# Inputs of VectorE moved to PSUM and a gate product moved to ScalarE, in the second part of a decoder block

## The chip, the core and the metric

One core of a Trainium2 chip. The time is the device time of one execution in microseconds (us); of several runs the median counts. Engines: TensorE (PE in the profile, PEld its weight loads), VectorE (DVE), ScalarE (ACT), GpSimd (POOL) and SyncE (SP, which issues most DMAs).

## The reference

A decoder block of 1024 tokens with 1024 features, all in float32: adaLN modulation, an input projection, a causal convolution beside an RWKV-7 time mixing, an output projection, and then a PEER mixer of 16384 experts. The last is what the change is about:

```python
q = (xc @ w_q).reshape(tc, PEER_HEADS, 2, PEER_DQ // 2)
s = jnp.einsum('thpd,hpkd->thpk', q, sub_keys)
...
best, pos = lax.top_k(cand.reshape(tc, PEER_HEADS, ...), PEER_TOPK)
gate = jax.nn.softmax(best, axis=-1)
ue = jnp.take(expert_u, expert, axis=0)
ve = jnp.take(expert_v, expert, axis=0)
h = jax.nn.gelu(jnp.einsum('thkd,td->thk', ue, xc), approximate=False)
return jnp.einsum('thk,thkd->td', gate * h, ve)
```

Each token has 8 heads of 16 experts: 128 rows of U (1024 values) whose dot products with the token go through Gelu, are multiplied with the gate, and weigh 128 rows of V.

## The kernel before, in words

The 1024 tokens are 8 tiles of 128. The first part of the kernel (to about 1900 us) does all of the block up to the choice of the experts. For the experts there are two ways, by tile:

- Tiles 0, 3, 6 and 7 are *gathered*. `stream_fetch` asks, with an indirect DMA of GpSimd's queue, for one row of U and V (2048 values) per token, 128 times per tile, into three buffers (`row`). `stream_use` makes the dot product of the U half with the tokens (`V.tensor_tensor_reduce`, shown as CUSTOM_DVE_ANT_0 and an accumulator read). `stream_add` has ScalarE make Gelu of the one column `hj`, VectorE multiply it with the gate, and VectorE add the V half times `hj` to `acc` (`scalar_tensor_tensor`, 128x1024). When that has ended, the buffer is free for a new gather. In the first part GpSimd makes a quarter of the dot products (`stream_useg`). After 128 rows, the tile's end transposes `acc` on TensorE into the bank `pD`, adds the residual and normalises.
- Tiles 1, 2, 4 and 5 (512 tokens) are *dense*: in the second part they go through all experts on TensorE. There are 128 blocks of 128 experts. Each operand is split into a high and a low part (type F32R), and each product is three matmuls: high by high, low by high and high by low. `stream_du` splits a block of U (`wh` on ScalarE, `wl` on GpSimd), `stream_dv` pieces of V (`vh`, `vl` likewise). `stream_mm` makes 24 matmuls of 512 columns into a bank `ph` (two of them); `stream_post` makes Gelu on ScalarE into `h` in SBUF, two products with the gates `gt` on VectorE, `ch` (ScalarE) and `cl` (VectorE); after 4 blocks `stream_mm` makes the 8 products with V, 12 matmuls each, into banks `po` (four of them), and `stream_sum` adds each to `accT` in SBUF on VectorE. The rows of the gathered tiles that are left (some 280 of 512) run beside it.

The streams are Python generators. `Issue.go` takes the stream whose next instruction can start first by a rough estimate; a `Wait` holds a stream back until a condition on the streams' counters holds. So the order of the instructions on each engine is fixed when the program is built. A tile with `bufs=n` takes its place from the n-th tile before, and waits on the chip until that one has been read.

[...] In the second part `pD` and `pC` have one each, `ph` two and `po` four.

Nearly all profile rows have the line L220, the helper that issues every operation; the names of the tiles tell them apart.

Of the kernel before, what the change touches and what calls it, by code (L numbers as in the profile page):

```python
# [19 lines left out]
T = 1024  # L20
D = 1024
# [7 lines left out]
def _groups():  # L29
    """The pairs (a, b) of ranks that can be among the 16 best sums, as rectangles (a0, na, b0, nb), in the order in  # L30
    which they are laid out: a pair has at least (a + 1)(b + 1) - 1 pairs before it that are not less, so that only
    those with (a + 1)(b + 1) <= 16 count, and among the 8 best are only those with (a + 1)(b + 1) <= 8."""
    out, ends, n = [], [], 0
    for lo, hi in ((0, TOPK // 2), (TOPK // 2, TOPK)):
        for a in range(hi):
            b0, b1 = lo // (a + 1), hi // (a + 1)
            if b0 == b1:
                continue
            if out and len(ends) == (lo > 0) and out[-1][2:] == [b0, b1 - b0] and out[-1][0] + out[-1][1] == a:
                out[-1][1] += 1  # L40
            else:
                out.append([a, 1, b0, b1 - b0])
            n += b1 - b0
        ends.append(n)
    return out, ends
# [9 lines left out]
# columns of the packed per-feature vectors  # L55
# [10 lines left out]
# tiles of 128 tokens whose experts are gathered; the others go through all experts on the tensor engine  # L66
GATHER = (0, 3, 6, 7)
GE = 4  # blocks of 128 experts whose results are added up in PSUM
RUN_EXPERTS = True
# what the issue of an instruction of a stream on an engine is put back by, in ns  # L70
# [4 lines left out]
HG = (2, 8)  # heads that are selected at a time, by tile  # L75
# by how many instructions those of a stream come before their place in the order of issue
# [3 lines left out]
HU = 2  # heads that are asked for before the tokens are put away for the experts  # L80
SHARE = 4  # of 16 experts, those whose products are GpSimd's in the first phase
# [3 lines left out]
# ---------------------------------------------------------------------------------------------------  # L85
# The order in which instructions are issued: several streams of instructions are written down as
# generators, and the stream whose next instruction can start first goes first, by a rough estimate of
# what each instruction takes. Only the order depends on the estimate.
# ---------------------------------------------------------------------------------------------------
# [87 lines left out]
class Issue:  # L177
# [56 lines left out]
    def transfer(self, ready, dur):  # L234
        """the end of a transfer in the first gap that holds it"""
# [14 lines left out]
    def go(self, streams, until=None):  # L250
        """streams: generators, the most urgent first; until: when to stop, if not at the end of all"""
# [31 lines left out]
def block_kernel(ctx, tc, xT, cols, ada_w, w_in, w0, w2a2, g2, w_out, w_q, keysT, peer_uv, peer_uT, outT, dbg=None):  # L283
# [17 lines left out]
    psumD = ctx.enter_context(tc.tile_pool(name="psumD", bufs=1, space=PSUM))  # L301
# [7 lines left out]
    psum = first.enter_context(tc.tile_pool(name="psum", bufs=1, space=PSUM))  # L309

# [15 lines left out]
    def pD():  # L326
        return tl(psumD, [128, 512], "pD", bufs=1)

# [48 lines left out]
    # cumulative sums within a chunk (s on partitions, t on the free axis), relative to the chunk's middle:  # L377
    # [s <= t - kind] - [s <= MID], kind 0 inclusive, 1 exclusive
# [15 lines left out]
    # masks of the grams: rows s (either half), columns t; 0: s < t, 1: s <= t  # L394
# [8 lines left out]
    # identity in chunk form [(c t), s]  # L403
# [3 lines left out]
    # level k of the inverse: t in the odd, s in the even half of the same block of 2^(k+1)  # L407
# [28 lines left out]
    # sigmoid(x) as (1 + tanh(x / 2)) / 2, whose table the scalar engine seldom has to change: the halves go  # L436
    # into what is multiplied with it
# [3 lines left out]
    # silu(c), each value along a row: the products with it come out on every partition  # L441
# [13 lines left out]
    # carried over the tokens  # L455
# [8 lines left out]
    def weights(src, wtag):  # L464
        """a block of weights in two pieces"""
# [37 lines left out]
    def rsqrt(out, t, x, eps):  # L503
        """out = (x + eps) ** -0.5: the table's value and one Newton step"""
# [5 lines left out]
    def mods(x, acol, shcol, n, pool, tag, ps):  # L510
        """x = rmsnorm(x) * acol + shcol in place, feature-major [128, 8, n]"""
        yield from norm(x, n, pool, tag, ps)
        yield from affine(x, acol, shcol)
# [29 lines left out]
    # ================= stream A: input projection and conv =================  # L543
    def stream_a():
        # the norm of the first tokens while the modulations are on their way
# [14 lines left out]
    def macro_a(t0, n, u):  # L560
# [19 lines left out]
        # blocks (wl|al), k0-3, r0-3, v0-3, gl with the token shift  # L580
        for m, b in enumerate((12, 4, 5, 6, 7, 0, 1, 2, 3, 8, 9, 10, 11, 13)):
            ps = yield from proj(b)
            # mu times the tokens, after the one before
# [12 lines left out]
        # gated input of the conv: blocks a_i, b_i  # L596
# [12 lines left out]
    # ================= stream L: conv, layer norm, silu =================  # L609
# [38 lines left out]
    # the taps of the conv, channel block by channel block: on the tensor engine as diagonal matrices, on the  # L648
    # scalar engine and GpSimd, or on the vector engine
# [42 lines left out]
    # ================= stream B: rwkv, 128 tokens at a time =================  # L692
# [8 lines left out]
    def have(i, n):  # L701
        """whether the first n blocks of the input projection are there for tile i"""
# [3 lines left out]
    def rwkv_tile(i):  # L706
# [18 lines left out]
        # cumulative decays  # L725
# [17 lines left out]
        # kk normalised per head  # L743
# [13 lines left out]
        # k * (1 + (a - 1) k_a)  # L757
# [8 lines left out]
        # alpha | rho and beta | kappa (chunk 1: kappa | beta)  # L766
# [9 lines left out]
        # grams: rows (beta|kappa), columns (alpha|rho)  # L776
# [20 lines left out]
        # token-major copies: v, beta|kappa, alpha  # L797
        UV = [rt("UV%d" % c, ("Pn", "Px")[c], (128, NH, 64)) for c in range(2)]

        def copies():  # L800
            for c in range(2):
                k0 = 64 - 64 * c
                pt = pB((128, 512))
                for p in range(4):
                    o, vi = pt[k0:k0 + 64, p * 128:(p + 1) * 128], v[:, p, c * C:(c + 1) * C]
                    if k0:  # a transpose can't write from partition 64 on
# [18 lines left out]
            # bonus  # L825
# [19 lines left out]
        # (I - L)^-1, both chunks at once, in blocks that double  # L845
# [29 lines left out]
        # M V, Z = T M V, W^T = alpha^T T^T  # L875
# [23 lines left out]
        # the chain over chunks  # L899
# [24 lines left out]
        # group norm per head, bonus, gate  # L924
# [21 lines left out]
    # ================= stream C: output projection, selection of the experts =================  # L946
# [10 lines left out]
    def macro_c(t0, n):  # L957
# [4 lines left out]
        if not t0:  # L962
            # the part of the conv, while the rwkv part is on its way
# [71 lines left out]
    # ================= stream D: selection =================  # L1035
# [26 lines left out]
    def top16(src, vals, idxs, n8, n):  # L1062
        """the 8 best of the first n8 values, then the 8 next of all n; overwrites src"""
# [6 lines left out]
    def select_experts(st, i, h0, hg):  # L1070
        """the experts and gates of the heads h0 .. h0 + hg - 1"""
# [5 lines left out]
        # a pair (a, b) of ranks can be among the 16 best only if (a + 1)(b + 1) <= 16  # L1077
# [56 lines left out]
    def selected(st, i):  # L1134
# [8 lines left out]
        # the selected pairs and gates with the 128 places on partitions, tokens along  # L1143
# [17 lines left out]
    # ================= stream G: gates of all experts for the tokens that aren't gathered =================  # L1161
    ONE = []  # a, b, token of the pair, whether of the late kind
    none = dict(made=[0, 0], used=[0, 0])

    def stream_g():
        for m, i in enumerate(DT_):
            yield Wait(lambda: done["sel"] > i)
            selT = SEL[i]["selT"]
            for ch in range(8):
                # in the places of stream A, once it has come to its end  # L1170
                late = int(done["yin"] == NT)
                qs = 4 if late else 2
                for t in range(16 * ch, 16 * ch + 16, qs):
# [8 lines left out]
                    # a: the gate where the first key is the place; b: 1 where the second key is,  # L1182
                    # on the scalar engine as |place - second key|, then 1 where that is 0
# [43 lines left out]
    # ================= streams of the gathered experts: fetch, products with the tokens, sums =================  # L1227
    ROW, DOT, USED, U2, X1, FIN = {}, {}, set(), {}, {}, set()
# [3 lines left out]
    def stream_fetch():  # L1232
        ring = []  # what tells whether the place of a row may be taken
# [3 lines left out]
        for m, i in enumerate(GT_):  # L1237
# [9 lines left out]
            # a place for the end of the tile  # L1247
# [6 lines left out]
    def stream_use():  # L1254
        """products of the experts with the tokens on the vector engine"""
        for m, i in enumerate(GT_):
# [3 lines left out]
            for n in range(m * 128, (m + 1) * 128):  # L1260
                yield Wait(lambda: done["fetch"] > n)
                if OWN[n]:
                    continue
                hj = tl(gat, [128, 1], "hj", bufs=2 * ROWS)
                row = ROW[n][:, 0:1024]
                yield V.tensor_tensor_reduce(row, row, U2[m], 1.0, 0.0, ALU.mult, ALU.add, hj)
# [3 lines left out]
    def stream_useg():  # L1270
        """the same on GpSimd and the scalar engine, for a part of the experts of the first phase"""
# [11 lines left out]
    def stream_add():  # L1283
        for m, i in enumerate(GT_):
            acc = None
            for j in range(128):
                n = m * 128 + j
                yield Wait(lambda: n in DOT and SEL[i].get("gates", 0) > j)
                if acc is None:
                    acc = tl(gat, [128, 8, 128], "acc")  # L1290
                    accf = acc.rearrange("p k t -> p (k t)")
# [4 lines left out]
                yield V.tensor_tensor(hj, hj, gate[:, j:j + 1], op=ALU.mult)  # L1296
                if j:
                    yield V.scalar_tensor_tensor(accf, row, hj, accf, op0=ALU.mult, op1=ALU.add)
                else:
                    yield V.tensor_scalar(accf, row, hj, None, op0=ALU.mult)  # L1300
                USED.add(n)
                done["used"] = n + 1
            # x + gt_ffn * out, feature-major, and the last norm
            yield Wait(lambda: done["x1"] > m)
            x1, sq = X1[m][:, 0], X1[m][:, 1]
            yield lock()
            done["lock"] = 1
            for h in range(2):
                ps = pD()
# [7 lines left out]
            ps = pD()  # L1317
# [254 lines left out]
```

## Time and profile before

| | |
|---|---|
| median of 3 runs | 3683.55 us (3681.07 to 3698.7) |
| span of the profiled execution | 3691.2 us; no other time of it is given |
| PE busy in the span | 3158.9 us, 86% |
| DVE | 3293.1 us, 89% |
| ACT | 1439.0 us, 39% |
| POOL | 2272.8 us, 62% |
| DMA | 923.02 MB, mean 250 GB/s |

Busy is the time in which the engine had an instruction under way, also one that stood still inside. The shares are of the whole span, which has two parts of a different kind: they have to be read per part, with the windows.

### The profile page before, as it was taken

Reading aid. Unit: us, or ns where it says so; the run is one execution under the profiler, and the core shown is the slowest. Engines: PE = TensorE matmul, PEld = TensorE weight load, DVE = VectorE, ACT = ScalarE, POOL = GpSimd, SP = SyncE. Lnnn points to the kernel's source line nnn. Section 1 sums busy time; section 2 is a strip of 40 time slices with the busy share of each in tenths; the row PEclk is TensorE's granted clock in tenths of the full one; section 3 lists DMA queues with packets and bytes.
Section 4 is the critical chain, followed back from the end, with each engine's and each line's share of the span. In section 5 each row is a group of like instructions: output and inputs, shape, how many; then the busy total and the mean of one; then the engine's idle time right before and its main releaser. Section 6 shows DMA issues by size and latency. Waiting matters only on the chain. (4 is left out here: it accounts for less than half of the span.)

```text
span 3691.2 us, 53824 instructions
## 1 busy us (share of the span) xinstructions
PE 3158.9 (86%) x18460; PEld 2544.7 (69%) x18460; DVE 3293.1 (89%) x6356; ACT 1439.0 (39%) x3315; POOL 2272.8 (62%) x2007
## 2 busy tenths in 40 slices
PE   5999998986999799767847789889889999889897
PEld 4788787765777577656746677667667777667675
DVE  5744989799698979988999999999999999999998
ACT  3545526436553436525642222222222232222222
POOL 1304647677675655567858766666666766666664
PEclk9788997988899889868878899999999999999998
DMA  6654776864676357657886788888888888888886
GB/s 208 207 171 156 282 248 235 300 211 175 235 283 228 129 177 248 230 178 271 288 303 217 245 277 282 285 269 294 277 289 284 290 283 298 285 291 281 286 280 226
DMA packets 423938, 923.02 MB, mean 250 GB/s; under 512 B 30449, under 2 KB 263025, under 8 KB 354033
## 3 DMA queue, kind: packets, MB, share of 16 engines
q0 software_dynamic: 73728, 536.90, 41.2%
q1 hardware_dynamic: 349936, 382.67, 32.0%
q8 instruction: 147, 2.41, 0.3%
q14 instruction: 127, 1.03, 0.1%
HBM read 873.33 MB, written 46.14 MB: 249 GB/s over the span
## 5 line engine op out<-in xcount | busy, mean ns | idle before, releaser
L220 POOL DMA_INDIRECT row<-in_peer_uv_dram,idx x512 | 670.4, 1309 | 723.5 <-DVE acc L220 504.9
L220 DVE CUSTOM_DVE_ANT_0 row<-row,u 128x1024 f32<-128x1024 f32 x457 | 705.8, 1545 | 36.1 <-DMA row<-in_peer_uv_dram,idx 34.7
L220 DVE SCALAR_TENSOR_TENSOR acc<-row,hj,acc 128x1024 f32<-128x1024 f32 x508 | 720.7, 1419 | 9.2
L220 ACT ACTIVATE hj<-hj 128x1 f32<-128x1 f32 x512 | 102.9, 202 | 1123.3 <-DVE hj L220 1122.0
L220 PE MATMUL po<-ch,vl 128*128 128x512 f32 x1024 | 427.8, 420 | 127.0 <-POOL vl L220 126.8
L220 PE MATMUL po<-ch,vh 128*128 128x512 f32 x1024 | 417.8, 409 | 37.1 <-ACT vh L220 21.2
L220 PE MATMUL po<-cl,vh 128*128 128x512 f32 x1024 | 414.6, 409 | 22.6 <-DVE cl L220 21.6
L220 POOL TENSOR_TENSOR vl<-v,vh 128x512 fp32r<-128x512 f32 x256 | 369.8, 1452 | 52.3 <-ACT vh L220 49.2
L220 PE MATMUL pA<-uA,wtA 128*128 128x256 f32 (+1 forms) x1760 | 352.9, 352 | 12.3 <-ACT xs L220 5.6
L220 DVE TENSOR_TENSOR hj<-hj,gate 128x1 f32<-128x1 f32 x512 | 291.3, 571 | 77.5 <-ACT hj L220 77.2
L220 POOL TENSOR_TENSOR wl<-w,wh 128x1024 fp32r<-128x1024 f32 x128 | 327.7, 2561 | 47.1 <-ACT wh L220 45.6
L220 PEld LDWEIGHTS po<-ch,vl 128*128 128x128 f32 x1024 | 200.4, 196 | 217.3 <-POOL vl L220 178.1
L220 POOL TENSOR_TENSOR cb<-cb,tap 128x256 f32<-128x256 f32 (+1 forms) x300 | 236.8, 790 | 161.8 <-ACT tap L220 139.0
L220 PE MATMUL ph<-uh,wh 128*128 128x512 f32 x1024 | 288.8, 416 | 43.6 <-ACT wh L220 40.0
L220 PEld LDWEIGHTS pA<-uA,wtA 128*128 128x128 f32 x1760 | 291.3, 200 | 46.9 <-ACT xs L220 7.2
L220 DVE TENSOR_TENSOR h<-h,gt 128x256 f32<-128x256 f32 x256 | 277.1, 1121 | 2.5 <-ACT h L220 2.3
L220 PE MATMUL pC<-uC,wtC 128*128 128x256 f32 (+1 forms) x1280 | 265.4, 362 | 15.8 <-ACT uC L220 6.0
L220 PEld LDWEIGHTS ph<-uh,wh 128*128 128x128 f32 x1024 | 209.2, 205 | 92.8 <-ACT wh L220 41.0
L220 PE MATMUL ph<-uh,wl 128*128 128x512 f32 x1024 | 267.4, 394 | 2.7 <-POOL wl L220 2.7
L220 PE MATMUL ph<-ul,wh 128*128 128x512 f32 x1024 | 268.3, 390 | 0.0
L220 PEld LDWEIGHTS po<-ch,vh 128*128 128x128 f32 x1024 | 199.2, 195 | 97.0 <-ACT vh L220 30.1
L220 PEld LDWEIGHTS po<-cl,vh 128*128 128x128 f32 x1024 | 200.3, 196 | 75.4 <-DVE cl L220 36.6
(299 smaller groups left out, 6486.3 us busy)
## 6 DMA issues: line engine op xcount, KB each, us to landing
v<-in_peer_uv_dram SPq DMA_DIRECT2D x256, 256.0 KB
w<-in_peer_uT_dram SPq DMA_DIRECT2D x128, 512.0 KB
wtA<-in_w_in_dram SPq DMA_DIRECT2D x220, 256.0 KB
wtC<-in_w_q_dram SPq DMA_DIRECT2D x160, 256.0 KB
Gd<-stg SPq DMA_DIRECT2D x32, 1024.0 KB
gt<-Gd SPq DMA_DIRECT2D x31, 1024.0 KB
wtC<-in_w_out_dram SPq DMA_DIRECT2D x80, 256.0 KB
wtC<-in_ada_w_dram SPq DMA_DIRECT2D x64, 256.0 KB
```

Source lines behind the costliest of these rows:

```text
L220: r = op.fn(*op.a, **op.k)
```

## The change

In the second part of the program:

- The tokens of a gathered tile are copied to PSUM once (`up`, two banks), and the dot products read them there. `acc` lies in PSUM too (`ap`, two banks), read and written in place; the last of the 128 sums writes to SBUF.
- Gelu of a dense block is made in place in the bank `ph`, the gates are multiplied in place, and `ch` and `cl` are made from there. The counter `d["P"]`, on which the next but one block's matmuls wait, goes up after `cl` instead of after Gelu.
- `po` has two banks, one of its own and `pC`, and the wait for `stream_sum` is two pieces shorter. The bank `pD` belongs to the first part alone; the end of a gathered tile in the second part uses `pO` without the lock.

In both parts the product of `hj` with the gate is on ScalarE, as an activation Copy whose scale is the gate. The change also takes out comments. Its core:

```diff
+    def pO(n):
+        return pC() if n % 2 else tl(second["psum"], [128, 512], "po", bufs=1)
...
 def stream_use():
+                if second and m not in UP:
+                    UP[m] = tl(second["psum"], [128, 1024], "up")
+                    yield A.copy(UP[m], U2[m])
                 hj = tl(gat, [128, 1], "hj", bufs=2 * ROWS)
                 row = ROW[n][:, 0:1024]
-                yield V.tensor_tensor_reduce(row, row, U2[m], 1.0, 0.0, ALU.mult, ALU.add, hj)
+                yield V.tensor_tensor_reduce(row, row, UP.get(m, U2[m]), 1.0, 0.0, ALU.mult, ALU.add, hj)
...
 def stream_add():
                 yield A.activation(hj, hj, AF.Gelu)
-                yield V.tensor_tensor(hj, hj, gate[:, j:j + 1], op=ALU.mult)
+                yield A.activation(hj, hj, AF.Copy, scale=gate[:, j:j + 1])
+                old, inp = acc, second and j < 127
+                if acc is None or inp != acc[1]:
+                    acc = (tl(second["psum"], [128, 1024], "ap") if inp else tl(gat, [128, 1024], "acc"), inp)
                 if j:
-                    yield V.scalar_tensor_tensor(accf, row, hj, accf, op0=ALU.mult, op1=ALU.add)
+                    yield V.scalar_tensor_tensor(acc[0], row, hj, old[0], op0=ALU.mult, op1=ALU.add)
...
-                ps = pD()
+                ps = pO(h) if late else pD()
...
 def stream_mm():
-                    yield Wait(lambda: d["V"] > o and d["S"] >= o - 3)
+                    yield Wait(lambda: d["V"] > o and d["S"] >= o - 1)
                     vh, vl = V_.pop(o)
-                    PO[o] = ps = tl(psum2, [128, 512], "po", bufs=4)[:, :NTD]
+                    PO[o] = ps = pO(o)[:, :NTD]
...
 def stream_post():
-            h = tl(dn, [128, NTD], "h", bufs=2)
-            yield A.activation(h, PH.pop(e), AF.Gelu)
-            d["P"] = e + 1
+            h = PH.pop(e)
+            yield A.activation(h, h, AF.Gelu)
...
             yield A.copy(ch, h)
             yield V.tensor_tensor(cl, h, ch, op=ALU.subtract)
             C_[e] = (ch, cl)
-            d["C"] = e + 1
+            d["P"] = d["C"] = e + 1
```

## Rows read from the trace of the kernel before

**Rows 1.** Windows: stretch, length, busy of each engine (instructions), PE clock, DMA share, GB/s

```profile
1600.00:1900.00 300.00, 221.63 (x1310) 194.57 (x1309) 275.04 (x767) 154.24 (x330) 221.46 (x228) 0.79 0.75 268
1940.00:3672.00 1732.00, 1532.29 (x6212) 1192.73 (x6213) 1689.01 (x1946) 477.25 (x963) 1154.59 (x733) 0.96 0.83 277
2200.00:3600.00 1400.00, 1253.74 (x5163) 980.77 (x5162) 1370.64 (x1549) 389.09 (x786) 924.74 (x564) 0.97 0.85 285
```

**Rows 2.** Costliest groups by shape, DVE, 2000 to 3600 us (count | busy, mean | idle before)

```profile
L220 DVE CUSTOM_DVE_ANT_0 row<-row,u 128x1024 f32<-128x1024 f32 x276 | 466.5, 1690 | 1.9 <-DMA row<-in_peer_uv_dram,idx 1.8
L220 DVE SCALAR_TENSOR_TENSOR acc<-row,hj,acc 128x1024 f32<-128x1024 f32 x273 | 391.0, 1432 | 7.7
L220 DVE TENSOR_TENSOR h<-h,gt 128x256 f32<-128x256 f32 x240 | 259.7, 1121 | 2.5 <-ACT h L220 2.3
L220 DVE TENSOR_TENSOR hj<-hj,gate 128x1 f32<-128x1 f32 x275 | 220.9, 804 | 19.5 <-ACT hj L220 19.4
L220 DVE TENSOR_TENSOR accT<-accT,po 128x512 f32<-128x512 f32 x234 | 157.0, 679 | 0.0
L220 DVE TENSOR_TENSOR cl<-h,ch 128x512 fp32r<-128x512 f32 x120 | 106.5, 903 | 0.8 <-ACT ch L220 0.7
L220 DVE DVE_READ_ACCUMULATOR2_ANT hj<- 128x1 f32 x276 | 22.0, 80 | 0.0
...
L220 DVE SCALAR_TENSOR_TENSOR x<-pD,modc,x 128x128 f32<-128x128 f32 x16 | 4.5, 338 | 0.0
```

**Rows 3.** Timeline, 2600 to 2632 us: start, duration, instruction

```profile
2602.82 1.21 DVE L220 CUSTOM_DVE_ANT_0 row<-row,u 128x1024 f32<-128x1024 f32 x1
...
2607.46 1.28 DVE L220 SCALAR_TENSOR_TENSOR acc<-row,hj,acc 128x1024 f32<-128x1024 f32 x1
...
2609.80 0.76 DVE L220 TENSOR_TENSOR h<-h,gt 128x256 f32<-128x256 f32 x2
...
2611.47 2.78 POOL L220 TENSOR_TENSOR wl<-w,wh 128x1024 fp32r<-128x1024 f32 x1
...
2611.92 3.42 DVE L220 CUSTOM_DVE_ANT_0 row<-row,u 128x1024 f32<-128x1024 f32 x1
...
2615.86 2.86 DVE L220 TENSOR_TENSOR hj<-hj,gate 128x1 f32<-128x1 f32 x1
2616.18 2.52 POOL L220 TENSOR_TENSOR vl<-v,vh 128x512 fp32r<-128x512 f32 x2
...
2622.05 0.16 DVE L220 TENSOR_TENSOR hj<-hj,gate 128x1 f32<-128x1 f32 x1 [0.27 <-ACT hj L220]
```

**Rows 4.** The same groups, POOL, 2000 to 3600 us

```profile
L220 POOL DMA_INDIRECT row<-in_peer_uv_dram,idx x277 | 393.5, 1421 | 434.1 <-DVE acc L220 403.7 <-DVE hj L220 16.1 <-issue 5.4
L220 POOL TENSOR_TENSOR vl<-v,vh 128x512 fp32r<-128x512 f32 x242 | 349.0, 1450 | 43.2 <-ACT vh L220 40.3
```

**Rows 5.** Waits, 2000 to 3600 us: who for whom, total us, times, longest

```profile
POOL row L220 <- DVE acc L220: 403.7, 198, 6.3
...
PE po L220 <- POOL vl L220: 121.5, 103, 3.8
```

**Rows 6.** Windows of 10 us, columns as in group 1

```profile
2490.00:2500.00 10.00, 9.59 (x42) 7.52 (x41) 9.93 (x14) 2.87 (x6) 5.45 (x4) 1.00 1.03 375
...
2640.00:2650.00 10.00, 10.00 (x45) 8.25 (x45) 10.00 (x13) 4.27 (x9) 4.24 (x3) 1.00 0.65 218
```

**Rows 7.** Groups by shape, DVE, 0 to 1900 us

```profile
L220 DVE TENSOR_TENSOR hj<-hj,gate 128x1 f32<-128x1 f32 x209 | 63.1, 306 | 56.1 <-ACT hj L220 55.9
...
L220 DVE SCALAR_TENSOR_TENSOR kk<-a,kk 128x512 f32<-128x512 f32 x8 | 5.4, 681 | 0.0
```

**Rows 8.** Groups by shape, ACT, 2000 to 3600 us

```profile
L220 ACT CAST ch<-h 128x512 fp32r<-128x512 f32 x120 | 72.2, 617 | 100.7 <-DVE h L220 56.2 <-DVE hj L220 33.9 <-issue 9.7
L220 ACT ACTIVATE h<-ph 128x512 f32<-128x512 f32 x119 | 70.5, 592 | 63.6 <-DVE cl L220 60.9 <-PE ph L220 2.6
L220 ACT ACTIVATE hj<-hj 128x1 f32<-128x1 f32 x275 | 55.8, 203 | 915.2 <-DVE hj L220 915.0
```

More of the change, by code (lines that the diff above doesn't have):

```diff
@@ L300, in block_kernel @@
     dram = ctx.enter_context(tc.tile_pool(name="dram", bufs=1, space=DRAM))
-    psumD = ctx.enter_context(tc.tile_pool(name="psumD", bufs=1, space=PSUM))
     psumC = ctx.enter_context(tc.tile_pool(name="psumC", bufs=1, space=PSUM))
@@ L309, in block_kernel @@
     psum = first.enter_context(tc.tile_pool(name="psum", bufs=1, space=PSUM))
+    psumD = first.enter_context(tc.tile_pool(name="psumD", bufs=1, space=PSUM))
+    second = {}
     def tl(pool, shape, name, tag=None, bufs=1, dt=F32):
@@ L1225, in stream_h @@
                 yield LD(Gd[m * 8 + ch], stg.rearrange("p i t -> p (i t)"))
-    ROW, DOT, USED, U2, X1, FIN = {}, {}, set(), {}, {}, set()
+    ROW, DOT, USED, U2, UP, X1, FIN = {}, {}, set(), {}, {}, {}, set()
     claim = dict(over=0)
@@ L1288, in stream_add @@
                 yield Wait(lambda: n in DOT and SEL[i].get("gates", 0) > j)
-                if acc is None:
-                    acc = tl(gat, [128, 8, 128], "acc")
-                    accf = acc.rearrange("p k t -> p (k t)")
+                if not j:
                     gate = SEL[i]["gate"].rearrange("p h k -> p (h k)")
@@ L1295, in stream_add @@
                 yield A.activation(hj, hj, AF.Gelu)
-                yield V.tensor_tensor(hj, hj, gate[:, j:j + 1], op=ALU.mult)
+                yield A.activation(hj, hj, AF.Copy, scale=gate[:, j:j + 1])
+                old, inp = acc, second and j < 127
+                if acc is None or inp != acc[1]:
+                    acc = (tl(second["psum"], [128, 1024], "ap") if inp else tl(gat, [128, 1024], "acc"), inp)
                 if j:
-                    yield V.scalar_tensor_tensor(accf, row, hj, accf, op0=ALU.mult, op1=ALU.add)
+                    yield V.scalar_tensor_tensor(acc[0], row, hj, old[0], op0=ALU.mult, op1=ALU.add)
                 else:
-                    yield V.tensor_scalar(accf, row, hj, None, op0=ALU.mult)
+                    yield V.tensor_scalar(acc[0], row, hj, None, op0=ALU.mult)
                 USED.add(n)
@@ L1305, in stream_add @@
             x1, sq = X1[m][:, 0], X1[m][:, 1]
-            yield lock()
-            done["lock"] = 1
+            acc = acc[0].rearrange("p (k t) -> p k t", k=8)
+            late = bool(second)
+            if not late:
+                yield lock()
+                done["lock"] = 1
             for h in range(2):
-                ps = pD()
+                ps = pO(h) if late else pD()
                 for k in range(4):
@@ L1316, in stream_add @@
                 yield A.activation(sq[:, 4 * h:4 * h + 4], x1[:, 4 * h:4 * h + 4], AF.Square)
-            ps = pD()
+            ps = pO(0) if late else pD()
             for k in range(8):
@@ L1321, in stream_add @@
             yield from rsqrt(rs, sq[:, 0, :], ps[:, 0:128], RMS_EPS)
-            done["lock"] = 0
+            if not late:
+                done["lock"] = 0
             for k in range(8):
@@ L1356, in block_kernel @@
     early = [st[k] for k in "abylgh"] + taps
-    iss.go(prefix + experts, until=lambda: all(u in iss.over for u in early) and done["ym"] == NT)
+    iss.go(prefix + experts, until=lambda: all(u in iss.over for u in early) and done["ym"] == NT and not done["lock"])
     claim["over"] = 1
@@ L1362, in block_kernel @@
     dn = ctx.enter_context(tc.tile_pool(name="dn", bufs=1))
-    psum2 = ctx.enter_context(tc.tile_pool(name="psum2", bufs=1, space=PSUM))
+    psum2 = second["psum"] = ctx.enter_context(tc.tile_pool(name="psum2", bufs=1, space=PSUM))
     NE = 128
@@ L1495, in stream_sum @@
             d["S"] = n + 1
-        rs = tl(dn, [128, NTD], "rsf", tag="h", bufs=2)
+        rs = tl(dn, [128, NTD], "rsf")
         yield from rsqrt(rs, accT[:, 0, :], ps, RMS_EPS)
```

## The prediction

> **What bounds the kernel now.** I read the windows first. From 1940 to 3672 us the second part runs: 128 blocks of 128 experts, each 24 matmuls into ph and 24 into po. In it VectorE is busy 1689 of 1732 us, in the steady stretch 1370.64 of 1400, TensorE 1253.74, ScalarE 389 and GpSimd 925 [rows 1]. So VectorE sets the pace. At 48 matmuls a block the 5163 of the steady stretch are 107.6 blocks, 13.0 us each (a few belong to the ends of tiles).
>
> The groups by shape say what VectorE does in 1600 us, about 123 such blocks [rows 2]. The reader should compare the two rows of 128x512 tensor_tensor: cl<-h,ch, with both inputs in SBUF, takes 903 ns in the mean, accT<-accT,po, with one in PSUM, 679. A product of 128x1 elements takes 804.
>
> The timeline shows why [rows 3]. The dot product takes 1.21 us at 2602.82 and 3.42 at 2611.92. GpSimd's wl had started at 2611.47 and ran until 2614.25; the long dot product ends 1.09 us after that. The gate product of one column, 0.16 us at 2622.05, took 2.86 from 2615.86, to 2618.72; vl ran on GpSimd until 2618.70. An instruction of VectorE with two SBUF inputs stands still until GpSimd's instruction has ended, and its time counts as busy. accT's does not: its 234 average 679 ns, and a 128x512 with two SBUF inputs that met little of GpSimd took 681 [rows 2, 7]. GpSimd stands behind in turn: it waits 403.7 us for acc before a gather, and its gathers average 1421 ns [rows 4, 5].
>
> **Part by part.** All per block, with 2.3 rows of experts a block (276 in 123 blocks, rounded up).
>
> The three kinds of PSUM inputs, priced as unblocked. Dot product 1.21 for 1.69, sum into acc 1.28 for 1.43, the h products 0.38 for 1.12 (the pair took 0.76), cl 0.68 (the length of accT) for 0.90 [rows 2, 3]. That takes 1.10, 0.34, 1.48 and 0.22 off VectorE, 3.1 us in all. A pointer in SBUF beside a PSUM input does not bring the block back: x<-pD,modc,x has both and averages 338 ns over 16 [rows 2].
>
> The gate product leaves VectorE: 2.3 x 0.80 = 1.8 us. ScalarE gets it, in the first part too. ScalarE's one-column Gelu takes 203 ns [rows 8]; with the gate as a pointer I take 0.3 (below by 203, above by the 592 of a whole 128x512 Gelu). Beside 389 us in 1400, that is 2.3 x 0.3 = 0.7 us of a ScalarE with some 9 us free per block, and the hop from ScalarE to VectorE stays one. Behind it in ScalarE's queue stand vh, wh, ch and h; each waits 0.3 us more at most, below what hides it.
>
> VectorE then needs 2.3 x (1.21 + 0.08 + 1.28) + 0.76 + 0.68 + 1.3 (accT) + 0.3 (the rest) = 9.0 us a block. It stops being the bound. The 0.08 is the accumulator's read behind each dot product [rows 2]; the 0.3 is my allowance.
>
> What is late next is TensorE. In a stretch without a gap it does 45 matmuls in 10 us at full granted clock [rows 6], 0.222 each, 10.67 a block. Its idle time now is (1400 - 1253.74) / 107.6 = 1.36 us a block, of which vl on GpSimd makes 121.5 / 123 = 0.99 [rows 1, 5]. GpSimd's vl averages 1450 ns and its gathers 1421 with VectorE in the way, and it waits 3.3 us a block for acc [rows 4, 5]; with VectorE free most of it should go. I let a third of the 0.99 stand, 0.33, and all the rest, 0.37, since two things of the change press there. First, ph is now worked on in place: its bank is given back after cl, not after Gelu. The chain Gelu 0.59, two h products 0.76, ch 0.62, cl 0.68 is 2.65 us without waits, and the next block's 24 matmuls cover 5.33 [rows 3, 8]. Second, po has two banks for four: VectorE must have drained one while the other's 12 matmuls run, 2.67 us, and its queue holds a dot product or a sum of 1.2 ahead. Both are hidden as long as VectorE has slack. So 10.67 + 0.33 + 0.37 = 11.37 us for 13.02, and 1.65 x 128 = 211 us gained.
>
> Writes of VectorE and ScalarE into PSUM don't occur before. From below I take the price of the same instruction into SBUF (a gain is possible, but no row has one), from above twice that, if reading and writing one bank took turns: 1.28 more for each sum, 0.38 more for each h product. I take the lower end, since reading PSUM alone cost nothing beside SBUF (679 and 681), and keep the upper as a rival.
>
> [...]
>
> DMA: 285 GB/s at a share of 0.85 rises to 327 at the new pace; 375 was reached over 10 us [rows 1, 6], and the dot products waited 1.8 us in all for their rows [rows 2]. I cost it at nothing; if that cover went, it is the first rival. The copies of the tokens to PSUM, once a tile, go beside other work.
>
> The end of a gathered tile now takes its banks from po: two such ends lie inside the second part, some 3 us each (eight sums of 0.34 ahead of the next po), 6 us lost. The first part loses 63 us of gate products on VectorE [rows 7]; VectorE is near its limit only in the last 300 us (275 busy), which hold about a sixth of it, so 10 us, between a loss of 20 by another order of issue and a gain of 40.
>
> Sum: 211 + 10 - 6 = 215 us. The profiled span is 3691.2 us, with no other time of that execution given; the median of the runs shown is 3683.55, 0.2% less, and I take the sum from the median: **3468 us**.
>
> **The rivals.** *The pace stays ragged*: orders on the engines are fixed beforehand, and VectorE, in order, stands behind a row that lands late, with h and cl behind it. TensorE then keeps its 1.36 us idle: 12.03 a block, 127 + 4 gained, 3553. For it speaks that DMA must move 15% more; against, the 1.8 us of waits.
>
> *TensorE goes dense*: 10.67 a block, 301 + 4 gained, 3379. For: GpSimd is the cause of most idle now. Against: the two new holds on banks.
>
> *VectorE stays the bound*, either because PSUM in place costs double, 9.0 + 2.3 x 1.28 + 0.76 = 12.7 us, or because one PSUM input does not free it and the wait passes from the gate product to the next instruction: the change then does not do what it says, and little more than 2.3 x 0.16 is saved. Both give 12.7 for 13.0, 38 us, some 3642. Against: accT's rows.
>
> *Slower*: the bank of ph. If the chain from Gelu to cl takes as long as VectorE's crowded queue can make it, TensorE waits for the bank in three blocks of four. It decides where the chain passes 5.33 us; to lose, the wait must make up 2.35 a block, so a chain of 5.33 + 2.35 x 4 / 3 = 8.5 us. With 9 us, a block is 10.67 + 3.67 x 0.75 = 13.4, 0.4 x 128 = 51 us more, 3735 with nothing else. Such a chain needs 6 us of waits in two visits to VectorE; at 9.0 us of 11.4 it is busy, but its longest single piece is 1.28.
>
> **How the numbers follow.** Forecast 0.60, ragged 0.20, dense 0.10, VectorE still the bound 0.06, slower 0.04. The range goes from 3365 (dense, with some of the first part's 40) to 3575 (ragged, with the first part's loss of 20); it leaves out the last two. A measurement here can tell about 0.5%, 18 us, from no change. All of the first four are faster by more: 0.95 with the last 0.01 of doubt set aside; of the rest 0.02 within, 0.03 slower.
>
> **What would show it.** VectorE's busy share in the second part falls to about 0.8; the dot product's mean to about 1.2 us, h's to 0.4, with no long ones; GpSimd's vl to below 1.35 and gathers to 1.0; TensorE above 0.93; ScalarE with 512 more one-column products. The forecast is wrong if VectorE's means don't fall, if TensorE's waits for cl or accT take the place of those for vl, or if the dot product waits for its row by tens of us.

## The result, and the profile after the change

The kernel became slower: 3994.5 us in the median of 4 runs (3982.52 to 4006.02) against 3689.39 for the kernel before (4 runs, 3681.07 to 3698.7). The ratio is 1.083, with a 95% interval of 1.0794 to 1.0865. The forecast was 3468 us, at 0.95 that it would be faster; it was wrong in sign. The profiled execution took 4000.64 us, its span 3998.9.

The page of the profile after the change: first the span in 40 equal slices of 100 us (busy share in tenths, and TensorE's granted clock), then one row of the costliest groups (count | busy, mean ns | idle time before, and what ended it).

```profile
PE   5999988969998978678306997019994069999998
...
DVE  5656888997798698889887676777666742222223
...
PEclk7799989968898887789657999559997579999999
...
L220 PE MATMUL po<-ident,acc 128*128 128x128 f32 x12 | 3.3, 435 | 501.1 <-DVE acc L220 501.1
```

TensorE has three holes, each one or two slices wide, in which its clock is down to 0.5, and a long dense stretch at the end in which VectorE is 0.2 busy. The last row names the holes: the twelve transposes of `acc` that go to `po` (twelve more go to `pC`), from the ends of the three gathered tiles that fall into the second part, stand behind 501.1 us of idle time. The waits, from 1960 to 3990 us (who for whom, total us, times, longest):

```profile
PE po L220 <- DVE acc L220: 501.1, 3, 198.6
POOL row L220 <- DVE ap L220: 386.6, 197, 6.0
...
PE ph L220 <- DVE cl L220: 11.6, 5, 4.7
...
PE pC L220 <- POOL vl L220: 6.4, 7, 1.3
```

Before, TensorE's largest wait was for vl, 121.5 us in 103 pieces [rows 5]. That one has gone, further than predicted (6.4 us for `pC` here and 1.2 for `po`, where a third was to stand). In its place there are three waits of up to 198.6 us.

What the engines do around a hole, in windows (columns as in [rows 1]): the stretch between two tile ends, the hole in it, and the end of the kernel.

```profile
2131.00:2679.00 548.00, 323.58 (x1364) 259.39 (x1362) 391.79 (x543) 154.11 (x402) 258.71 (x211) 0.80 0.90 315
...
2480.00:2679.00 199.00, 0.75 (x4) 0.29 (x2) 142.65 (x176) 31.30 (x119) 55.44 (x58) 0.51 0.89 318
3300.00:3900.00 600.00, 600.00 (x2648) 496.12 (x2647) 159.81 (x277) 181.64 (x277) 274.73 (x167) 1.00 0.41 121
```

And the timeline there (start, duration, instruction, idle time before and its releaser): what VectorE does in the hole, and how the hole ends.

```profile
2567.02 1.29 DVE L220 SCALAR_TENSOR_TENSOR ap<-row,hj,ap 128x1024 f32<-128x1024 f32 x1 [0.60 <-ACT hj L220]
2568.22 1.21 DVE L220 CUSTOM_DVE_ANT_0 row<-row,up 128x1024 f32<-128x1024 f32 x1
2569.36 0.08 DVE L220 DVE_READ_ACCUMULATOR2_ANT hj<- 128x1 f32 x1
2570.04 1.29 DVE L220 SCALAR_TENSOR_TENSOR ap<-row,hj,ap 128x1024 f32<-128x1024 f32 x1 [0.60 <-ACT hj L220]
...
2679.39 1.11 PE L220 MATMUL po<-ident,acc 128*128 128x128 f32 x4 [198.64 <-DVE acc L220]
2680.30 1.06 PE L220 MATMUL pC<-ident,acc 128*128 128x128 f32 x4
2682.86 0.79 PE L220 MATMUL po<-ch,vh 128*128 128x512 f32 x1 [1.50 <-DVE x L220]
```

In the hole VectorE does rows one after another, about 3 us each, and no block. TensorE waits for the tile's last sum, makes the eight transposes, and goes on with the products of V 3.5 us later, into the bank that the transposes had. From the third tile end at 3233.86 us on no rows are left: the last 68 blocks (by the `cl` of VectorE) run alone. From 3300 to 3900 us TensorE is 600.00 of 600 us busy, 600 / 2648 x 48 = 10.88 us a block, while DMA stands at 0.41.

How many blocks and rows lie between two tile ends, from the groups on VectorE: first the kernel after, 2131 to 2679 us, then the kernel before, 2213 to 2949 us.

```profile
L220 DVE CUSTOM_DVE_ANT_0 row<-row,up 128x1024 f32<-128x1024 f32 x128 | 155.8, 1217 | 48.3 <-DMA row<-in_peer_uv_dram,idx 47.8
L220 DVE TENSOR_TENSOR cl<-ph,ch 128x512 fp32r<-128x512 f32 x28 | 18.7, 686 | 15.3 <-ACT ch L220 15.3
```

```profile
L220 DVE CUSTOM_DVE_ANT_0 row<-row,u 128x1024 f32<-128x1024 f32 x128 | 217.6, 1700 | 0.1
L220 DVE TENSOR_TENSOR cl<-h,ch 128x512 fp32r<-128x512 f32 x54 | 47.3, 893 | 0.0
```

A tile's 128 rows go with 54 blocks before, 2.4 rows a block, and with 28 after, 4.6 a block. Beside rows a block takes 12.1 us (794 matmuls between 2200 and 2400 us), so 28 blocks are some 340 us; the 128 rows take the 548.

The prices themselves came out as predicted. The groups by shape of the kernel after, 2000 to 3600 us, of VectorE, GpSimd and ScalarE:

```profile
L220 DVE SCALAR_TENSOR_TENSOR ap<-row,hj,ap 128x1024 f32<-128x1024 f32 x280 | 360.4, 1287 | 106.4 <-ACT hj L220 103.7 <-DVE ap L220 0.5
L220 DVE CUSTOM_DVE_ANT_0 row<-row,up 128x1024 f32<-128x1024 f32 x283 | 344.3, 1217 | 101.6 <-DMA row<-in_peer_uv_dram,idx 100.5
L220 DVE TENSOR_TENSOR ph<-ph,gt 128x256 f32<-128x256 f32 x181 | 78.0, 431 | 204.8 <-ACT ph L220 202.6
L220 DVE TENSOR_TENSOR cl<-ph,ch 128x512 fp32r<-128x512 f32 x91 | 61.0, 688 | 54.9 <-ACT ch L220 54.9
...
L220 POOL DMA_INDIRECT row<-in_peer_uv_dram,idx x287 | 273.6, 953 | 449.8 <-DVE ap L220 386.6 <-DMA row<-in_peer_uv_dram,idx 23.5 <-PE ph L220 10.0
L220 POOL TENSOR_TENSOR vl<-v,vh 128x512 fp32r<-128x512 f32 x184 | 236.7, 1292 | 161.0 <-ACT vh L220 158.5 <-DMA v<-in_peer_uv_dram 1.5
...
L220 ACT ACTIVATE hj<-hj,gate 128x1 f32<-128x1 f32 x289 | 85.1, 295 | 8.3
```

The means 1432, 1690, 1121 and 903 ns of [rows 2] are now 1287, 1217, 431 and 688; the gathers and vl of [rows 4] went from 1421 and 1450 to 953 and 1292.

### The profile page after: what moved, and what is told of

It reads as the page before. It is cut to its first block, busy times and chain, and to the rows that moved or that the text cites. A ratio compares the mean times of both kernels' runs of the same rounds, so it can differ in the third digit from the quotient of the medians.

```text
span 3998.9 us, 54133 instructions
## 1 busy us (share of the span) xinstructions
PE 3089.8 (77%) x18460; PEld 2538.0 (63%) x18460; DVE 2726.1 (68%) x5824; ACT 1591.8 (40%) x3837; POOL 2109.4 (53%) x2024
## 3 DMA queue, kind: packets, MB, share of 16 engines
q1 hardware_dynamic: 349936, 382.67, 29.9%
## 4 chain that ended last, share of the span: by engine, by line
PE 40%; DVE 18%; DMA 14%; issue 12%; POOL 10%; ACT 5%; SPq 1%; POOLq 0%; DVEq 0%; ACTq 0%
PE pC L220 10%; PE ph L220 10%; PE pB L220 9%; DMA row<-in_peer_uv_dram,idx 7%; PE po L220 5%; PE pA L220 5%; POOL row L220 4%; DMA v<-in_peer_uv_dram 3%; DVE acc L220 3%; DMA w<-in_peer_uT_dram 3%; POOL wl L220 2%; DVE row L220 2%; DVE cb L220 2%; DVE onea L220 2%; POOL vl L220 2%
## 5 line engine op out<-in xcount | busy, mean ns | idle before, releaser
L220 POOL DMA_INDIRECT row<-in_peer_uv_dram,idx x512 | 542.8, 1060 | 709.0 <-DVE ap L220 386.6
L220 POOL TENSOR_TENSOR vl<-v,vh 128x512 fp32r<-128x512 f32 x256 | 330.6, 1298 | 246.0 <-ACT vh L220 242.1
L220 DVE SCALAR_TENSOR_TENSOR ap<-row,hj,ap 128x1024 f32<-128x1024 f32 x280 | 360.4, 1287 | 106.4 <-ACT hj L220 103.7
L220 DVE CUSTOM_DVE_ANT_0 row<-row,up 128x1024 f32<-128x1024 f32 x283 | 344.3, 1217 | 101.6 <-DMA row<-in_peer_uv_dram,idx 100.5
L220 PE MATMUL po<-ident,acc 128*128 128x128 f32 x12 | 3.3, 435 | 501.1 <-DVE acc L220 501.1
L220 DVE SCALAR_TENSOR_TENSOR acc<-row,hj,acc 128x1024 f32<-128x1024 f32 x224 | 315.8, 1410 | 50.9 <-ACT hj L220 50.0
L220 DVE TENSOR_TENSOR ph<-ph,gt 128x256 f32<-128x256 f32 x256 | 110.4, 431 | 343.4 <-ACT ph L220 340.1
L220 ACT CAST vh<-v 128x512 fp32r<-128x512 f32 x256 | 156.1, 618 | 333.5 <-PE po L220 111.7
L220 ACT CAST wh<-w 128x1024 fp32r<-128x1024 f32 x128 | 134.1, 1048 | 349.9 <-PE ph L220 304.5
L220 DVE CUSTOM_DVE_ANT_0 row<-row,u 128x1024 f32<-128x1024 f32 x171 | 236.0, 1382 | 40.5 <-DMA row<-in_peer_uv_dram,idx 40.5
L220 PEld LDWEIGHTS pC<-uC,wtC 128*128 128x128 f32 x1280 | 220.0, 207 | 45.8 <-ACT s L220 11.9
```

The costliest lines, as they stand in the source:

```text
L220: r = op.fn(*op.a, **op.k)
```

## The experiments

**Theory A**: the end of a gathered tile now takes places in the ring of `po` banks. The program is built in two steps. `Issue.go` writes the instructions down, and a ring gives out its places in that order; then the framework's scheduler (the kernel opens it with `schedule_with_timeline_sim=True`, L1568) sets the queue of each engine, free to move what no tile ties. Counted as the program writes them down, the ends of the second and third gathered tile stand behind 33 and 61 blocks before and behind 32 and 61 after: 28 or 29 blocks for 128 rows in both kernels. Before, the end had `pD` to itself, and the scheduler could slide it, to 54 blocks a tile. In the ring of `po` it cannot: every later product with V takes its bank after the end, and TensorE, in order, stands still behind the transposes until the rows are done, 198.6 us at the longest. **The rivals**: the loss comes not from the order, but from the longer hold on `ph`, from the work in place in PSUM, from two banks in `po` for four, or from a tile end that stands early in TensorE's order whatever bank it has.

**The tile end in banks of its own.** Undoes that part alone; the end uses the two banks of `ap`, which the tile no longer needs then.

```diff
+            own = tl(second["psum"], [128, 1024], "ap") if late else None
             for h in range(2):
-                ps = pO(h) if late else pD()
+                ps = own[:, 512 * h:512 * h + 512] if late else pD()
...
-            ps = pO(0) if late else pD()
+            ps = own[:, 0:512] if late else pD()
```

> The changed kernel, but the end of a gathered tile in the second part works in the two banks of ap, which are free by then, instead of in the banks of the second product. Theory A (the order in which po and pC are handed out is fixed when the program is written; there the tile's end stands after 28 blocks, the rows need longer, and all later second products stand behind it): TensorE's wait of 501 us for acc falls below 20 us, rows and blocks run side by side to the end, some 11.8 us a block, total 3490 us (3440 to 3550). Theory B (two banks for po and the longer hold of ph slow TensorE whatever the tile's end does): the waits move to accT and cl, total over 3900 us. Theory C (the tile's end is early in TensorE's order, whatever bank it has): still 3 waits of 100 to 200 us for acc, total about 4000 us.

Measured: 3549.03 us (3535.99 to 3552.45), ratio to the kernel before 0.9609 (0.9581 to 0.9637). The wait for `acc` is gone from TensorE's list. Its largest from 2000 us on, and the steady stretch (columns as in [rows 1]):

```profile
PE pC L220 <- ACT vh L220: 17.0, 11, 3.7
PE po L220 <- ACT vh L220: 16.8, 8, 6.3
```

```profile
2200.00:3400.00 1200.00, 1132.16 (x4801) 912.81 (x4801) 842.59 (x1227) 430.45 (x976) 718.77 (x536) 0.97 0.90 317
```

That is 445 us less than the kernel after, by three lines. Both kernels write the tile ends down behind the same number of blocks (32 and 61 for the second and third). On the chip, by the `cl` that VectorE has done, the three ends stand behind 4, 32 and 60 blocks in the kernel after and behind 16, 72 and 124 in this one: with a bank of its own the end slides, in the ring it does not. The time is at the upper edge of what was expected: a block takes 1200 / 4801 x 48 = 12.0 us, not 11.37.

**The shared end alone, in the kernel before.** Nothing else of the change; `po` keeps its four banks. As in the change, the end does not take the lock there; the diff leaves those lines out.

```diff
-                ps = pD()
+                ps = tl(second["psum"], [128, 512], "po", bufs=4) if late else pD()
...
-            ps = pD()
+            ps = tl(second["psum"], [128, 512], "po", bufs=4) if late else pD()
```

> The kernel before, with the end of a gathered tile in the second part in the four banks of po instead of in its own bank, and nothing else: no PSUM input, no gate on ScalarE. Theory A: the same waits as in the changed kernel appear, TensorE waits over 400 us for acc, total 4050 us (3950 to 4250). Theories B and C: about 3690 us, as before.

Measured: 4047.62 us in one run, where the kernel before took 3692.26: 355 us more. Its waits, 2000 to 4000 us:

```profile
PE po L220 <- DVE acc L220: 503.8, 3, 200.0
PE po L220 <- POOL vl L220: 62.0, 44, 3.6
```

The three waits are there without any input in PSUM, with the gate on VectorE and four banks in `po`. Together the two runs show the cause from both sides.

**The end left in `po`, the rows paced.** `stream_fetch` may issue a row only when enough blocks have been issued, so that the written order has 2.3 rows a block.

```diff
+                if second:
+                    second.setdefault("n0", n)
+                    yield Wait(lambda: "d" not in second or second["d"]["H"] >= 128
+                               or 10 * (n - second["n0"]) <= 23 * second["d"]["H"] + 60)
```

> The changed kernel with its banks as they are, but a gathered row of the second part is written down only when its share of the dense blocks has been (2.3 rows a block, 6 ahead). Theory A: the tile's ends come after some 56 blocks instead of 28, so the wait for acc shrinks to under 80 us in all (some 17 rows still stand alone ahead of the first end), total 3540 us (3480 to 3620). Theory B: about 4000 us, since the banks are the same.

Measured: 3648.22 us (3625.84 to 3654.06), ratio 0.9865 (0.9828 to 0.9902). The waits fell from three and 501.1 us to one (TensorE, from 2000 us on):

```profile
PE po L220 <- DVE acc L220: 68.4, 1, 68.4
PE po L220 <- ACT ch L220: 39.9, 12, 4.3
PE po L220 <- DVE accT L220: 32.3, 26, 3.4
```

The three ends stand behind 8, 64 and 120 blocks on the chip. Theory A was right in direction and on the wait, but 108 us too hopeful in time and outside its own range: 68.4 us are left at the first tile end, at 2153.67 us, and the waits for `ch` and `accT` are longer than with the end in `ap` (39.9 and 32.3 us for 12.2 and 14.9); why was not traced. Still, the order as written is what makes the large waits, for nothing else was changed here, and a bank of its own is the better cure.

**The gate product alone, and the sum alone, in the kernel before.** The first is the one line of `stream_add` with ScalarE's Copy. The second puts the sum into PSUM, `po` on two banks, the end in `pD`.

> The kernel before with the gate product on ScalarE and nothing else. If the blocked time of the gate product passes on to the next instruction of VectorE with two SBUF inputs: VectorE saves only 0.16 us a row, total 3640 us (3600 to 3680), the mean of the sum into acc rising above 1.6 us. If it goes away: 1.8 us a block less, 3450 us.

> The kernel before with the sum into acc in PSUM in the second part and nothing else (po with two banks to make room, the tile's end in its own bank as before, gate product on VectorE, dot product and h from SBUF). If time that is no longer spent behind GpSimd in one instruction passes on to the next with two SBUF inputs: only some 0.1 to 0.3 us a row go, total 3650 us (3600 to 3700), and the means of dot product and h rise. If each kind of instruction keeps its own share: 3685 minus 0.15 x 2.3 x 128 = 3640 us too, but the means of the others stay. The total does not tell these apart, the means do.

Measured: 3669.85 us (ratio 0.9938, 0.9918 to 0.9959) and 3607.27 (0.9779, 0.9758 to 0.9801). The groups on VectorE, 2000 to 3600 us, first with the gate moved, then with the sum in PSUM:

```profile
L220 DVE CUSTOM_DVE_ANT_0 row<-row,u 128x1024 f32<-128x1024 f32 x279 | 504.2, 1808 | 16.7 <-DMA row<-in_peer_uv_dram,idx 16.6
L220 DVE SCALAR_TENSOR_TENSOR acc<-row,hj,acc 128x1024 f32<-128x1024 f32 x279 | 490.5, 1758 | 49.5 <-ACT hj L220 49.1
```

```profile
L220 DVE CUSTOM_DVE_ANT_0 row<-row,u 128x1024 f32<-128x1024 f32 x289 | 500.6, 1732 | 18.4 <-DMA row<-in_peer_uv_dram,idx 17.9 <-issue 0.4
L220 DVE SCALAR_TENSOR_TENSOR ap<-row,hj,ap 128x1024 f32<-128x1024 f32 x284 | 365.4, 1287 | 7.7
...
L220 DVE TENSOR_TENSOR hj<-hj,gate 128x1 f32<-128x1 f32 x289 | 163.7, 567 | 21.9 <-ACT hj L220 21.8
```

The gate product took 804 ns of VectorE [rows 2]; without it the sum, now next behind GpSimd, takes 326 more and the dot product 118 more. More than half of the blocked time passed on, as the third rival of the prediction had it. The expectation of 3640 was too low by 30; the first ph matmul starts at 1964.6 us for 1940.1 before, so in its profile 24 us of that lie in the first part. With the sum in PSUM little passed on: the sum fell by 145 ns and the gate's product by 237, while the dot product rose by 42. The time, 43 us under the middle of what was expected, is within its range.

**What is left in the version with its own banks.** Four kernels from the first experiment's: five `v` tiles for three; the dot product from SBUF; the gate product back on VectorE; Gelu to `h` in SBUF, so that `ph` is free after Gelu. A fifth joins the first and the last.

```diff
-            v = tl(dn, [128, GE, 128], "v", bufs=3)
+            v = tl(dn, [128, GE, 128], "v", bufs=5)
```

```diff
-                if second and m not in UP:
+                if False:
```

```diff
-                yield A.activation(hj, hj, AF.Copy, scale=gate[:, j:j + 1])
+                yield V.tensor_tensor(hj, hj, gate[:, j:j + 1], op=ALU.mult)
```

```diff
-            h = PH.pop(e)
-            yield A.activation(h, h, AF.Gelu)
+            h = tl(dn, [128, NTD], "h", bufs=2)
+            yield A.activation(h, PH.pop(e), AF.Gelu)
+            d["P"] = e + 1
...
-            d["P"] = d["C"] = e + 1
+            d["C"] = e + 1
```

> The kernel of e1_end_in_ap with five places for the pieces of V on their way instead of three. There ScalarE waited 116 us in 1200 for pieces of V to land. If they are late because they are asked for late: that wait falls below 40 us, a block goes from 12.0 to 11.6 us, total 3500 us (3470 to 3530). If they are late because the DMA engines are full (share 0.90): total as e1_end_in_ap, 3549 us, give or take 20.

> The kernel of e1_end_in_ap with the tokens of the dot products in SBUF again (no copy to up). The dot product's mean goes from 1217 to 1650 ns, 1.0 us a block more on VectorE, which is busy 0.70 of the time there. If that slack hides it: 3549 us, give or take 20. If it delays GpSimd and what waits for both: 3610 us (3580 to 3650).

> The kernel of e1_end_in_ap with the gate product on VectorE again, in both parts. It is then one of the few instructions left there with two SBUF inputs, and waits for GpSimd's split instructions: mean 800 ns, 1.8 us a block on VectorE. If the slack hides it: 3549 us, give or take 20. If it does not: 3620 us (3580 to 3660).

> The kernel of e1_end_in_ap with Gelu writing to SBUF again, so that the gate products of a dense block and cl have two SBUF inputs, and the bank of ph is given back after Gelu. If the longer hold of ph is what keeps a block at 12.0 us: faster, 3490 us (3450 to 3530). If the stand behind GpSimd weighs more: h's mean rises from 431 to about 1000 ns, VectorE 1.4 us a block more, total 3590 us (3550 to 3640).

> The kernel of e9_h_in_sbuf with five places for V on their way as well. In e6_v_ahead and e9_h_in_sbuf TensorE is busy 0.985 of the steady stretch each, at 11.1 us a block; the floor of 48 matmuls is 10.87 us, as the changed kernel shows once its rows are done. If the two removed the same idle time: 3455 us (3435 to 3475). If they add up: 3370 us.

| kernel | us | ratio to before, 95% |
|---|---|---|
| tile end in `ap` | 3549.03 | 0.9609 (0.9581 to 0.9637) |
| and five `v` tiles | 3459.48 | 0.9391 (0.9359 to 0.9423) |
| and dot product from SBUF | 3541.3 | 0.9598 (0.9566 to 0.9631) |
| and gate product on VectorE | 3548.76 | 0.9618 (0.9582 to 0.9655) |
| and `h` in SBUF | 3459.09 | 0.9382 (0.9348 to 0.9416) |
| and `h` in SBUF, five `v` tiles | 3468.63 | 0.9392 (0.9355 to 0.9428) |

The steady stretch with five `v` tiles, then with `h` in SBUF:

```profile
2200.00:3300.00 1100.00, 1082.79 (x4742) 889.66 (x4741) 820.04 (x1209) 423.12 (x956) 708.28 (x527) 1.00 0.97 339
```

```profile
2200.00:3300.00 1100.00, 1083.76 (x4738) 887.48 (x4737) 964.38 (x1194) 429.49 (x944) 712.24 (x521) 1.00 0.95 334
```

Both bring a block to 1100 / 4742 x 48 = 11.1 us. How long ScalarE's vh waited for the load of `v` between 2200 and 3300 us, in the version with its own banks, with five tiles, and with `h` in SBUF:

```profile
ACT vh L220 <- DMA v<-in_peer_uv_dram: 99.6, 35, 7.8
...
ACT vh L220 <- DMA v<-in_peer_uv_dram: 28.0, 14, 5.8
...
ACT vh L220 <- DMA v<-in_peer_uv_dram: 17.8, 10, 5.0
```

TensorE's own waits for vh and vl in that stretch are 40.8 us of its 62.5 us of waits in the first of the three; with five tiles 2.4 are left. So late pieces of V made most of TensorE's idle 0.68 us a block, and both edits take away the same thing: together they gain nothing more. Why the longer hold of `ph` makes V's loads late was not traced.

The other two hardly changed the time (8 us less and none), though they put blocked time back. The groups on VectorE, 2200 to 3300 us, with the dot product from SBUF, then with the gate on VectorE:

```profile
L220 DVE CUSTOM_DVE_ANT_0 row<-row,u 128x1024 f32<-128x1024 f32 x218 | 328.8, 1508 | 48.9 <-DMA row<-in_peer_uv_dram,idx 45.0 <-DMA u<-u2d 3.6
...
L220 POOL DMA_INDIRECT row<-in_peer_uv_dram,idx x219 | 294.8, 1346 | 161.6 <-DVE ap L220 130.2 <-issue 9.5 <-DVE hj L220 3.5
```

```profile
L220 DVE TENSOR_TENSOR hj<-hj,gate 128x1 f32<-128x1 f32 x213 | 217.6, 1022 | 21.6 <-ACT hj L220 20.6
```

That VectorE, busy 842.59 of 1200 us, simply has the slack to hide them is not what the waits show. TensorE's waits for vh, 29.9 us in this stretch with the end in `ap`, are down to 8.1 and 1.5, and its waits for `accT`, 10.6 us there, have gone up in their place. First with the dot product from SBUF, then with the gate on VectorE:

```profile
PE po L220 <- DVE accT L220: 32.3, 17, 3.6
...
PE po L220 <- DVE accT L220: 42.0, 16, 6.1
```

With the gate on VectorE two effects in the time cancel besides, as the last experiment shows.

**Five `v` tiles in the kernel before.** The same edit, where VectorE is the bound.

> The kernel before with five places for V on their way and no other change. If VectorE bounds it, as its busy share of 0.98 says: no change, 3690 us, give or take 20. If the late V pieces were the bound all along and PSUM did little: 3600 us.

Measured: 3685.16 us in 10 runs, ratio 0.9988 (0.9971 to 1.0005): no change. The loads matter only once VectorE is out of the way.

**The gate product by part.** The first ph matmul, in the profile of each kernel, starts at 1929.6 to 1940.1 us in the five kernels so far with the gate product on VectorE in the first part (1940.1 before) and at 1955.9 to 1964.6 in the eight that have it on ScalarE (1960.0 after). From first to last ph, though, the version with its own banks takes 1539.1 us with ScalarE and 1555.2 with VectorE (one profile each). So the last kernel takes each where it is better, with five `v` tiles:

```diff
-                yield A.activation(hj, hj, AF.Copy, scale=gate[:, j:j + 1])
+                yield A.activation(hj, hj, AF.Copy, scale=gate[:, j:j + 1]) if second else \
+                    V.tensor_tensor(hj, hj, gate[:, j:j + 1], op=ALU.mult)
```

> The kernel with the tile ends in the banks of ap and five v tiles, with the product of hj and gate on VectorE in the first part and on ScalarE in the second. Theory A: the product on ScalarE is what delays the first part (first ph matmul at 1955 to 1965 us in all kernels that have it there, at 1930 to 1940 in all that have it on VectorE); here it starts at 1930 to 1940, the second part takes what it took (from the first ph to the end 1493.5 us), and the time is 3434 us (3422 to 3446), ratio 0.932. Theory B: the delay belongs to the order of issue of each program and is chance: the start stays near 1960 and the time near 3459, ratio 0.939.

Measured: 3430.01 us in 5 runs (3413.44 to 3439.45), ratio 0.9297 (0.9274 to 0.932), the fastest of all, 261 us faster than before. The instances of the ph matmuls, in that kernel and in the kernel after (durations min/median/max ns, first to last start):

```profile
L220 PE MATMUL ph<-uh,wh x1024: 387/389/796, 1921.2 to 3358.8; 128*128 128x512 f32 x171
```

```profile
L220 PE MATMUL ph<-uh,wh x1024: 387/389/797, 1960.0 to 3948.0; 128*128 128x512 f32 x171
```

The start moved as theory A had it, by more than expected. What in the first part makes ScalarE's product late (its queue, or the other order of issue) was not traced.

## Why the prediction was wrong

The step that failed is the one on the end of a gathered tile: "two such ends lie inside the second part, some 3 us each (eight sums of 0.34 ahead of the next po), 6 us lost". It priced the work between the transposes and the next `po`; the trace shows that work, 3.5 us from 2679.39 to 2682.86. It left out what the transposes themselves wait for, a tile's last sum. In the kernel before that was no question of banks: the transposes came when `acc` was ready, and in the second part TensorE idled 2.0 us for them at most:

```profile
2949.18 0.95 PE L220 MATMUL pD<-ident,acc 128*128 128x128 f32 x4 [2.01 <-DVE acc L220]
```

The step took it for granted that this would stay so; but a shared ring writes the end into the order of the blocks, as the rough estimates of `Issue.go` have it, and nothing in the prediction asked what order that is. There were also three such ends among the blocks, not two: before, the third stood behind the last block, at 3668.87 us. It forecast 6 us and came to 501.1.

The second term that was wrong is the first part: a gain of 10, between a loss of 20 and a gain of 40. It was a loss of 20, the bound: the first ph matmul starts at 1960.0 us for 1940.1. 495 + 30 = 525 us are nearly all of the 526 between 3468 and 3994.5, but that is partly chance, as the blocks outside the holes ran at two paces, 12.1 us beside rows and 10.9 alone, and not at 11.37.

Point by point:
- **VectorE stops being the bound**: right. 842.59 of 1200 us, 0.70, with the tile end in its own banks; 0.8 had been forecast.
- **One PSUM input frees VectorE of GpSimd**: right (1217, 431, 688 ns for a forecast of 1.21, 0.38, 0.68). The h product was priced from a pair at 0.76 [rows 3]; it takes 0.43.
- **PSUM in place at the lower end**: right, 1287 ns for 1.28; nothing like the doubling that the third rival needed.
- **The gate at 0.3 us on ScalarE**: right, 295 ns. That ScalarE hides it in the first part too was not: [rows 7] were read for what VectorE gains, not for who waits.
- **vl below 1.35, gathers at 1.0**: right, 1292 and 953 ns.
- **11.37 us a block**: the idle part came out in size (0.70 forecast, 0.68 measured in the first experiment), but by luck: vl, which was to make 0.33 of it, made 10.9 us in 100 blocks, and the largest share was vh, which waits for late pieces of V. The busy part was mis-sized: 10.67 forecast, 1132.16 / 4801 x 48 = 11.32 measured. 45 matmuls in a window of 10 us count to 0.222 us each; 2648 in 600 us are 0.227, 10.88 a block. The stretch of the first experiment had a granted clock of 0.97, not 1.00, which by an estimate makes 10.88 / 0.97 = 11.22 of the 11.32. The time of that experiment, 3549, is near the first rival's 3553, by luck too: the rival had 10.67 busy and 1.36 idle. The cover it named, DMA, did give way, but in pieces of V and not in rows.
- **The slower rival**, by the bank of ph: wrong mechanism. TensorE waited 11.6 us for cl in all, where the rival needed more than 2.35 a block, some 300 us.

An input in PSUM was priced like one in SBUF, and the medians of the kernel before and the kernel after agree within 15 ns. For the two that write to SBUF they are 683 and 691 ns (cl) and 1218 and 1215 (the dot product); for the two that work in place in PSUM 417 and 432 (the product with gt) and 1284 and 1290 (the sum).

## What to carry to other kernels

Where two streams share a ring of buffers, the ring makes one order of both, and an in-order engine enforces it (TensorE here, with 501.1 us of waits in the kernel after and 503.8 with the shared end alone): before a buffer is lent to another stream, count in the program how much of the one stands between two items of the other, and compare with the rates that the trace shows. Price a step that is moved into a queue by what it waits for, not only by what it does. And once the bound is removed, look again at settings that made no difference before: the depth of `v` was worth nothing with VectorE as the bound and 90 us in the version with the tile end in `ap`.

## What the runs showed of the hardware

- Reading and writing PSUM in place costs VectorE little over SBUF: 1290 ns for 1284 (128x1024), 432 for 417 (128x256), in medians. ScalarE's Gelu in place took 580 ns in the mean, for 592 into SBUF [rows 8].
- GpSimd's gathers themselves are slowed beside VectorE instructions with two SBUF inputs, and nearly all of it comes with the dot product: 1421 ns in the mean before, 953 after, 1346 with only the dot product back in SBUF, but 976 with the h products and cl back there and 949 with the gate product back. Which step of a gather stood still no run shows.
- DMA held a share of 0.97 and 339 GB/s over 1100 us beside dense matmuls; the best stretch of 10 us before had 375 [rows 6].
